# Weighted sum of expert outputs: a ring of token slots, interleaved VectorE sums, weights loaded once, 2 MiB stores, and three terms of the last eight tokens on TensorE

## The chip, the cores and the metric

The kernel runs on one core of a Trainium2 chip; the other cores are idle. The metric is the device time in microseconds (us) of one execution. Before the change three timed runs gave 721.29, 721.71 and 721.99 us; their median, 721.71 us, is the time to compare with.

## The reference

For 16 x 1024 = 16384 tokens there are eight expert rows of 512 float32 values and eight weights. The output row of a token is the weighted sum of its eight rows:

```python
def reference(expert_outputs, combine_weights):
    # expert_outputs (16, 1024, 8, 512) f32, combine_weights (16, 1024, 8) f32
    weights = combine_weights[..., np.newaxis]
    return np.sum(expert_outputs * weights, axis=2).astype(np.float32)
```

The core reads 268.4 MB of expert rows and 0.5 MB of weights, and writes 33.6 MB.

## The kernel before

A token of 16 KB (eight experts, 2 KB each) lies in one SBUF partition. The kernel cuts the tokens into 64 steps of 256: partition p of step n holds the two neighbouring tokens 256n + 2p and 256n + 2p + 1, so a load (line 56) is 4 MiB, 32 KB for each partition, and the whole of it is one contiguous piece of DRAM. The last two steps (`K_TAIL`) are loaded as two DMAs of 2 MiB, one for each j (line 59). Loads of even steps are issued by SyncE (SP), those of odd steps by ScalarE (ACT); each of the two has a DMA queue of its own. The 8 KB of weights of a step come by a small DMA from GpSimd (line 60). Four input buffers are used, and step n + 3 is loaded while step n is worked on.

For each token slot j of a step, VectorE makes the first product with a `tensor_scalar` (line 77) and adds the seven others with one `scalar_tensor_tensor` each (line 83): out = row times weight plus the sum so far, in one instruction over 128 partitions by 512 columns. Each sum is a chain of eight dependent instructions, and the second token's chain begins after the first's. The 512 KB of a step are then stored (line 92) by the queue that did not load this step, 4 KB for each partition.

The last two steps, 62 and 63, are different (lines 94 to 141). ScalarE multiplies experts 4 to 7 into bfloat16 (line 111), VectorE sums experts 0 to 3 in float32 (lines 116 and 122), adds the four products in bfloat16 (lines 130 and 135) and adds both halves (line 138). SP stores every half step by itself, 256 KB (line 141).

The order on each engine's instruction stream comes from the tile framework: it orders the instructions by a schedule of its own and sets the semaphores between them. A DMA is issued when the waits of its instruction have passed; what stands behind it on the same engine's stream waits with it. The waits follow the regions that instructions read and write, not whole tiles: at the end of the run ScalarE works on one half of a step while the other half is still under way.

Of the kernel before, what the change touches and what calls it, by code (L numbers as in the profile page):

```python
# [1 line left out]

# [4 lines left out]


@with_exitstack  # L10
def kernel(
    ctx: ExitStack,
    tc: tile.TileContext,
    expert_outputs: bass.AP,
    combine_weights: bass.AP,
    out: bass.AP,
):
    nc = tc.nc
    fp32 = mybir.dt.float32
    bf16 = mybir.dt.bfloat16  # L20

    B, S, E, D = expert_outputs.shape
    T = B * S
    P = 128
    J = 2
    n_steps = T // (P * J)

    eo_blk = expert_outputs.rearrange("b s e d -> (b s) e d").rearrange(
        "(n p j) e d -> n p j e d", p=P, j=J
    )  # L30
    w_blk = combine_weights.rearrange("b s e -> (b s) e").rearrange(
        "(n p j) e -> n p j e", p=P, j=J
    )
    o_blk = out.rearrange("b s d -> (b s) d").rearrange(
        "(n p j) d -> n p j d", p=P, j=J
    )

    in_pool = ctx.enter_context(tc.tile_pool(name="in_pool", bufs=4))
    w_pool = ctx.enter_context(tc.tile_pool(name="w_pool", bufs=4))
    out_pool = ctx.enter_context(tc.tile_pool(name="out_pool", bufs=4))  # L40
    prod_pool = ctx.enter_context(tc.tile_pool(name="prod_pool", bufs=2))

    ES = E // 2
    K_TAIL = 2

    load_engines = [nc.sync, nc.scalar]

    LA = 3
    in_tiles: list[bass.AP | None] = [None] * n_steps
    w_tiles: list[bass.AP | None] = [None] * n_steps  # L50

    def issue_load(m: int) -> None:
        in_t = in_pool.tile([P, J, E, D], fp32, name="in_t")
        w_t = w_pool.tile([P, J, E], fp32, name="w_t")
        if m < n_steps - K_TAIL:
            load_engines[m % 2].dma_start(out=in_t, in_=eo_blk[m])
        else:
            for j in range(J):
                load_engines[m % 2].dma_start(out=in_t[:, j], in_=eo_blk[m, :, j])
        nc.gpsimd.dma_start(out=w_t, in_=w_blk[m])  # L60
        in_tiles[m] = in_t
        w_tiles[m] = w_t

    for m in range(min(LA, n_steps)):
        issue_load(m)

    for n in range(n_steps):
        if n + LA < n_steps:
            issue_load(n + LA)
        if n >= n_steps - K_TAIL:  # L70
            continue
        in_tile = in_tiles[n]
        w_tile = w_tiles[n]
        acc = out_pool.tile([P, J, D], fp32)

        for j in range(J):
            nc.vector.tensor_scalar_mul(  # L77
                out=acc[:, j, :],
                in0=in_tile[:, j, 0, :],
                scalar1=w_tile[:, j, 0:1],  # L80
            )
            for e in range(1, E):
                nc.vector.scalar_tensor_tensor(  # L83
                    out=acc[:, j, :],
                    in0=in_tile[:, j, e, :],
                    scalar=w_tile[:, j, e : e + 1],
                    in1=acc[:, j, :],
                    op0=mybir.AluOpType.mult,
                    op1=mybir.AluOpType.add,
                )  # L90

        load_engines[(n + 1) % 2].dma_start(out=o_blk[n], in_=acc)  # L92

    tail_steps = list(range(n_steps - K_TAIL, n_steps))
    tail_accs = {}
    tail_prods = {}
    for n in tail_steps:
        acc = out_pool.tile([P, J, D], fp32, name="acc")
        prods = prod_pool.tile([P, J, E - ES, D], bf16, name="prods")
        tail_accs[n] = acc  # L100
        tail_prods[n] = prods

    for j in range(J):
        for n in tail_steps:
            in_tile = in_tiles[n]
            w_tile = w_tiles[n]
            acc = tail_accs[n]
            prods = tail_prods[n]

            for e in range(ES, E):  # L110
                nc.scalar.mul(  # L111
                    out=prods[:, j, e - ES, :],
                    in_=in_tile[:, j, e, :],
                    mul=w_tile[:, j, e : e + 1],
                )
            nc.vector.tensor_scalar_mul(  # L116
                out=acc[:, j, :],
                in0=in_tile[:, j, 0, :],
                scalar1=w_tile[:, j, 0:1],
            )  # L120
            for e in range(1, ES):
                nc.vector.scalar_tensor_tensor(  # L122
                    out=acc[:, j, :],
                    in0=in_tile[:, j, e, :],
                    scalar=w_tile[:, j, e : e + 1],
                    in1=acc[:, j, :],
                    op0=mybir.AluOpType.mult,
                    op1=mybir.AluOpType.add,
                )
            nc.vector.tensor_add(  # L130
                out=prods[:, j, 0:2, :],
                in0=prods[:, j, 0:2, :],
                in1=prods[:, j, 2:4, :],
            )
            nc.vector.tensor_add(  # L135
                out=prods[:, j, 0, :], in0=prods[:, j, 0, :], in1=prods[:, j, 1, :]
            )
            nc.vector.tensor_add(  # L138
                out=acc[:, j, :], in0=acc[:, j, :], in1=prods[:, j, 0, :]
            )  # L140
            nc.sync.dma_start(out=o_blk[n, :, j], in_=acc[:, j, :])


# [1 line left out]
_INS = ['expert_outputs', 'combine_weights']  # L145
_OUTS = [((16, 1024, 512), 'float32')]


# [23 lines left out]
```

## Time and profile before

| | |
|---|---|
| timed runs | 721.29, 721.71, 721.99 us |
| span of the profiled execution, first to last instruction | 720.4 us |
| VectorE busy | 644.4 us (89%) |
| ScalarE busy | 11.4 us (2%) |
| GpSimd busy | 35.8 us (5%), of which 35.6 us are the 64 weight loads of line 60 |
| TensorE | not used |
| DRAM traffic | 268.96 MB read, 33.55 MB written, 420 GB/s over the span |
| L83, 868 scalar_tensor_tensor | mean 743 ns |
| L77, 124 tensor_scalar | mean 482 ns |

The profile is of one execution; the page gives its span, and the three timed runs lie 0.9 to 1.6 us above that span. "Busy" is the time in which an engine executed instructions. A DMA's packets are worked off by 16 DMA engines; the DMA share is their mean busy share. Successive VectorE instructions overlap a little: fourteen of line 83 take 9.36 us in the timeline, 0.66 us from start to start, although each is shown as 743 ns long. Below, this distance from start to start is called a step.

### The profile page before, as it was taken

How to read it: one execution, taken by the hardware profiler on the slowest of the kernel's cores; microseconds unless marked ns; L12 is line 12 of the kernel's file. 1: busy time of each engine (PE TensorE's matmuls, PEld its weight loads, DVE VectorE, ACT ScalarE, POOL GpSimd, SP SyncE). 2: the span in 40 equal slices, each digit the busy share in tenths (PEclk: the TensorE clock that was granted, in tenths of full speed). 3: DMA queues.
4: the chain of work that ended last, by engine and by line, in shares of the span. 5: the costliest groups of instructions: out<-in, count | busy, mean ns of one | idle time of the engine just before them, and what ended most of it. 6: DMA issues, size and time to landing. Idle time of an engine off the chain costs nothing.

```text
span 720.4 us, 1532 instructions
## 1 busy us (share of the span) xinstructions
DVE 644.4 (89%) x1020; ACT 11.4 (2%) x17; POOL 35.8 (5%) x68
## 2 busy tenths in 40 slices
DVE  0799999999998999989998999989998999999977
ACT  0000000000000000000000000000000000000023
POOL 1000000000000000000000000000000000000000
DMA  9999999999999999999999999999999999999993
GB/s 380 437 416 451 427 426 430 427 424 439 443 431 426 426 423 431 438 436 434 431 423 426 435 430 442 432 424 427 430 429 432 442 431 428 430 425 428 433 359 120
DMA packets 21068, 302.63 MB, mean 420 GB/s; under 512 B 3136, under 2 KB 4160, under 8 KB 12608
## 3 DMA queue, kind: packets, MB, share of 16 engines
q1 hardware_dynamic: 9792, 151.52, 49.2%
q10 hardware_dynamic: 9216, 150.47, 48.9%
q0 software_dynamic: 2048, 0.53, 0.3%
q14 instruction: 12, 0.10, 0.0%
HBM read 268.96 MB, written 33.55 MB: 420 GB/s over the span
## 4 chain that ended last, share of the span: by engine, by line
DMA 63%; DVE 35%; issue 1%; DVEq 0%; SPq 0%
DMA out_dram<-acc 56%; DVE acc L83 30%; DMA in_t<-in_expert_outputs_dram 8%; DVE acc L77 3%; DVE acc L122 1%; DVE acc L138 0%; DVE prods L130 0%; DVE acc L116 0%; DVE prods L135 0%; DVEq L77 0%; DVEq L116 0%; SPq L92 0%
## 5 line engine op out<-in xcount | busy, mean ns | idle before, releaser
L83 DVE SCALAR_TENSOR_TENSOR acc<-in_t,w_t,acc 128x512 f32<-128x512 f32 x868 | 580.1, 743 | 0.0
L77 DVE TENSOR_SCALAR acc<-in_t,w_t 128x512 f32<-128x512 f32 x124 | 54.6, 482 | 66.3 <-DMA in_t<-in_expert_outputs_dram 43.4
L60 POOL DMA_DIRECT2D w_t<-in_combine_weights_dram x64 | 35.6, 556 | 637.7 <-DVE acc L83 636.9
L111 ACT ACT_TABLE_LOAD x1 | 1.3, 1283 | 690.6 <-DMA in_t<-in_expert_outputs_dram 690.6
L111 ACT ACTIVATE prods<-in_t,w_t 128x512 bf16<-128x512 f32 x16 | 10.1, 709 | 9.0 <-DMA in_t<-in_expert_outputs_dram 9.0
L122 DVE SCALAR_TENSOR_TENSOR acc<-in_t,w_t,acc 128x512 f32<-128x512 f32 x12 | 8.9, 745 | 0.0
L116 DVE TENSOR_SCALAR acc<-in_t,w_t 128x512 f32<-128x512 f32 x4 | 1.9, 481 | 5.3 <-DMA out_dram<-acc 5.3
L138 DVE TENSOR_TENSOR acc<-acc,prods 128x512 f32<-128x512 f32 x4 | 2.8, 688 | 0.0
L130 DVE TENSOR_TENSOR prods<-prods 128x1024 bf16<-128x1024 bf16 x4 | 2.7, 683 | 0.0
L135 DVE TENSOR_TENSOR prods<-prods 128x512 bf16<-128x512 bf16 x4 | 1.7, 417 | 0.0
L156 POOL MEMSET const-float32-0.0<- 128x1 f32 x1 | 0.1, 99 | 0.2 <-issue 0.2
L156 POOL MEMSET const-bfloat16-1.0<- 128x1 bf16 x1 | 0.1, 102 | 0.0
L156 POOL MEMSET const-float32-1.0<- 128x1 f32 x1 | 0.1, 99 | 0.0
L156 POOL MEMSET const-uint8-127<- 128x1 uint8 x1 | 0.1, 99 | 0.0
## 6 DMA issues: line engine op xcount, KB each, us to landing
in_t<-in_expert_outputs_dram ACTq DMA_DIRECT2D x31, 4096.0 KB, 33.5
in_t<-in_expert_outputs_dram SPq DMA_DIRECT2D x31, 4096.0 KB, 33.3
out_dram<-acc ACTq DMA_DIRECT2D x31, 512.0 KB, 33.5
out_dram<-acc SPq DMA_DIRECT2D x31, 512.0 KB, 33.4
in_t<-in_expert_outputs_dram SPq DMA_DIRECT2D x2, 2048.0 KB, 31.2
in_t<-in_expert_outputs_dram ACTq DMA_DIRECT2D x2, 2048.0 KB, 13.9
w_t<-in_combine_weights_dram POOLq DMA_DIRECT2D x64, 8.0 KB, 6.9
out_dram<-acc SPq DMA_DIRECT2D x4, 256.0 KB, 3.0
```

The costliest lines, as they stand in the source:

```text
L60: nc.gpsimd.dma_start(out=w_t, in_=w_blk[m])
L77: nc.vector.tensor_scalar_mul(out=acc[:, j, :], in0=in_tile[:, j, 0, :], scalar1=w_tile[:, j, 0:1],)
L83: nc.vector.scalar_tensor_tensor(out=acc[:, j, :], in0=in_tile[:, j, e, :], scalar=w_tile[:, j, e : e + 1], in1=acc[:, j, :], op0=mybir.Al ...
L111: nc.scalar.mul(out=prods[:, j, e - ES, :], in_=in_tile[:, j, e, :], mul=w_tile[:, j, e : e + 1],)
L116: nc.vector.tensor_scalar_mul(out=acc[:, j, :], in0=in_tile[:, j, 0, :], scalar1=w_tile[:, j, 0:1],)
L122: nc.vector.scalar_tensor_tensor(out=acc[:, j, :], in0=in_tile[:, j, e, :], scalar=w_tile[:, j, e : e + 1], in1=acc[:, j, :], op0=mybir.Al ...
L130: nc.vector.tensor_add(out=prods[:, j, 0:2, :], in0=prods[:, j, 0:2, :], in1=prods[:, j, 2:4, :],)
L135: nc.vector.tensor_add(out=prods[:, j, 0, :], in0=prods[:, j, 0, :], in1=prods[:, j, 1, :])
L138: nc.vector.tensor_add(out=acc[:, j, :], in0=acc[:, j, :], in1=prods[:, j, 0, :])
L156: nc = _bacc.Bacc("TRN2", target_bir_lowering=False, num_devices=1)
```

## The change

The kernel's middle is rewritten.

- **Layout.** Partition p now holds eight neighbouring tokens of each of 16 blocks (`G = 8`, 1024 tokens a block), 128 tokens in all, numbered i = 0 to 127 along the partition. A load is still two tokens for each partition, 4 MiB, 32 KB from each of 128 places in DRAM, but these places are now 128 KB apart.
- **Ring.** One tile `ring` has ten token slots; token i uses slot i % 10. Five loads can be in flight or in use, where it was four. All loads are issued by SP. Tokens 126 and 127 come in two and four pieces.
- **Weights.** All 0.5 MB are loaded by the first DMA of SP, in runs of 256 bytes.
- **First product.** ScalarE writes expert 0's product of each token into `acc`, one pair ahead of VectorE.
- **Two chains in turn.** VectorE adds experts 1 to 7 to the two tokens of a pair alternately.
- **Stores.** ScalarE issues one 2 MiB store for every eight tokens (16 KB for each partition), then one of 1 MiB for tokens 120 to 123; SP issues one of 512 KB for 124 and 125 and two of 256 KB for 126 and 127.
- **Last eight tokens.** For tokens 120 to 127 ScalarE makes three 128x128 float32 diagonal matrices from the weights, and TensorE sums experts 0 to 2 in PSUM with three float32 matmuls of 512 columns. VectorE adds experts 3 to 7, the first of them onto the sum in PSUM. The bfloat16 tail is gone.

`pin` keeps an instruction behind all that was written earlier for the same engine. The core of the diff, with the removed middle left out:

```diff
-    J = 2
-    n_steps = T // (P * J)
+    G = 8
+    N = T // (P * G)
+    T_P = N * G
+    SLOTS = 10
+    PE_TOKENS = 8
+    PE_EXPERTS = 3
...
+    x = expert_outputs.rearrange("b s e d -> (b s) e d").rearrange(
+        "(n p g) e d -> n p g e d", p=P, g=G
+    )
...
+    ring = one.tile([P, SLOTS, E, D], fp32, name="ring")
+    acc = one.tile([P, 2 * G, D], fp32, name="acc")
+    w_t = one.tile([P, T_P, E], fp32, name="w_t")
+    ident = one.tile([P, P], fp32, name="ident")
...
+    for t in range(BULK, T_P - 2, 2):
+        loads += [(t, 2, 0, E)]
+    loads += [(T_P - 2, 1, 0, 4), (T_P - 2, 1, 4, 8)]
+    loads += [(T_P - 1, 1, 0, 3), (T_P - 1, 1, 3, 5), (T_P - 1, 1, 5, 7), (T_P - 1, 1, 7, 8)]
...
+    def first(i):
+        s, a = i % SLOTS, i % (2 * G)
+        if i < T_P - PE_TOKENS:
+            pin(nc.scalar.mul(out=acc[:, a], in_=ring[:, s, 0], mul=w_t[:, i, 0:1]))
+            return
+        ps = ps_pool.tile([P, D], fp32, name="ps")
+        for e in range(PE_EXPERTS):
+            diag = diag_pool.tile([P, P], fp32, name="diag")
+            pin(nc.scalar.mul(out=diag, in_=ident, mul=w_t[:, i, e : e + 1]))
+            nc.tensor.matmul(
+                ps, lhsT=diag, rhs=ring[:, s, e], start=e == 0, stop=e == PE_EXPERTS - 1
+            )
+        sums[i] = ps
+
+    def term(i, e):
...
+            before, e0 = (sums[i] if e == PE_EXPERTS else acc[:, a]), PE_EXPERTS
+        if e >= e0:
+            pin(
+                nc.vector.scalar_tensor_tensor(
+                    out=acc[:, a],
+                    in0=ring[:, s, e],
+                    scalar=w_t[:, i, e : e + 1],
+                    in1=before,
...
+    pin(nc.sync.dma_start(out=w_t.rearrange("p (n g) e -> p n (g e)", g=G), in_=w))
+    make_identity(nc, ident)
+    load_until(SLOTS - 2)
+    for i in (0, 1):
+        first(i)
+    for i in range(0, T_P, 2):
+        load_until(i + SLOTS)
+        for k in (i + 2, i + 3):
+            if k < T_P:
+                first(k)
+        for e in range(E):
+            for k in (i, i + 1):
+                term(k, e)
+        end = i + 2
+        if end <= T_P - G and end % G == 0:
+            store(end - G, G, nc.scalar)
+        elif end == T_P - 4:
+            store(end - 4, 4, nc.scalar)
+        elif end == T_P - 2:
+            store(end - 2, 2, nc.sync)
+        elif end == T_P:
+            store(end - 2, 1, nc.sync)
+            store(end - 1, 1, nc.sync)
```

`load_until(t)` issues, in order, the loads of all tokens below t that are not yet issued; `store(i, m, queue)` stores m tokens from token i on.

## The prediction

> **What bounds the kernel now.** I read the page's slices and queues first, then the busy times by stage, then the waits of VectorE, and last the timeline of the end. From the page:
>
> ```profile
> DVE  0799999999998999989998999989998999999977
> ...
> DMA  9999999999999999999999999999999999999993
> ...
> q1 hardware_dynamic: 9792, 151.52, 49.2%
> q10 hardware_dynamic: 9216, 150.47, 48.9%
> q0 software_dynamic: 2048, 0.53, 0.3%
> ```
>
> VectorE looks full, but the 16 DMA engines are fuller: the three queues' packets fill 98.4% of the span. The table by stage has length, then busy us of VectorE, ScalarE and GpSimd, clock, DMA share, GB/s:
>
> ```profile
> 0.00:2.00 2.00, 0.00 (x0) 0.00 (x0) 0.96 (x6) 1.00 0.70 197
> 2.00:30.00 28.00, 7.06 (x12) 0.00 (x0) 1.50 (x3) 1.00 0.98 418
> ...
> 200.00:400.00 200.00, 183.10 (x289) 0.00 (x0) 9.65 (x18) 1.00 1.01 431
> ...
> 685.00:690.00 5.00, 5.00 (x9) 0.00 (x0) 0.00 (x0) 1.00 0.90 378
> 690.00:692.00 2.00, 2.00 (x4) 1.42 (x2) 0.00 (x0) 1.00 0.53 125
> 692.00:704.00 12.00, 6.66 (x13) 5.17 (x9) 0.00 (x0) 1.00 0.94 366
> 704.00:721.00 17.00, 12.01 (x21) 4.83 (x8) 0.00 (x0) 1.00 0.28 107
> ```
>
> From 30 to 685 us the share is 1.01 at 431 GB/s: DMA is the bound, and VectorE waits for it (183 of 200 us busy). VectorE's waits say so too:
>
> ```profile
> DVE acc L77 <- DMA in_t<-in_expert_outputs_dram: 43.4, 25, 22.9
> DVE acc L77 <- DMA out_dram<-acc: 22.9, 24, 1.9
> ```
>
> Past 685 us the DMA engines run dry while the computation ends. The timeline shows how:
>
> ```profile
> 690.72 0.82 ACTq L59 DMA_DIRECT2D in_t<-in_expert_outputs_dram  x2
> ...
> 708.41 2.56 ACT L111 ACTIVATE prods<-in_t,w_t 128x512 bf16<-128x512 f32 x4 [2.14 <-DMA in_t<-in_expert_outputs_dram]
> ...
> 715.36 0.69 DVE L138 TENSOR_TENSOR acc<-acc,prods 128x512 f32<-128x512 f32 x1
> ```
>
> The last two loads are issued at 690.72, when little else is under way; the last lands at 708.41; VectorE ends at 716.05; the span ends 4.35 us later (store and closing).
>
> So the span has three terms. By the packet records of the trace (duration by size), a packet of 32 KB takes 1213 ns, 16 KB 611, 8 KB 309, 4 KB 159, 2 KB 86, 512 B 27, and one of the 16 completion writes of a DMA 9: about 8.4 ns each plus 0.0368 ns a byte. All packets together are 709.4 us on each of 16 engines, which at the overlap of the middle (100.65 us of packets in 100 us) is 704.8 us. The first data packets start at 1.9 us. The rest, 720.4 - 704.8 - 1.9 = **13.7 us, is idle DMA**, all of it after 685 us.
>
> **The change, part by part.** *DMA work.* Stores: 32 MiB went as 4 KB and 2 KB packets, 81.7 us on each engine; after it, 15 x 128 packets of 16 KB x 611 ns / 16 = 73.3, 128 of 8 KB 2.5, 128 of 4 KB 1.3, 256 of 2 KB 1.4: 78.4. Loads: 623.8 in all, some of the last 16 KB packets being slow (mean 703 ns); after it, 63 x 128 x 1213 ns / 16 = 611.4, plus tokens 126 and 127 in 8, 6, 4 and 2 KB packets 10.1, plus 1.2 for slow first packets as now: 622.6. Weights: 1024 packets of 512 B, 1.7, against 2048 of 256 B, by the fit 17.8 ns each, 2.3. Completion writes: 3136 of 9 ns, 1.8, against 89 DMAs x 16, 0.8. With 0.4 for instructions: 704.5, in place of 709.4; divided by 1.0065, **700.0 us, 4.8 us less**.
>
> *One load queue.* All loads stand in SP's queue, behind no store. From 694 to 698 us q10 alone moved 430 GB/s, so one queue fills the engines; I cost it at nothing. If it did not, four loads in flight (39 us of data) could not help. The ring frees two slots when a pair is done, 10 us after its landing; those four loads hide that.
>
> *Loads 128 KB apart in place of 32 KB.* No row has this distance. Below: no gain, since the packets' 1213 ns have no spread (the 90th percentile is 1213 in nearly every stretch of 40 us). Above: the slow 16 KB packets at the end, 703 against 611 ns, 15%, which would be 90 us. I take nothing, since 1213 ns is the row of nearly all packets, and keep a rival. The Trainium skill speaks against this edit: "DMA: Bandwidth & Descriptors", section "Latency and other measured facts", lists DRAM copies at 512 KB between the partitions' rows at 207 GB/s, at 2 MiB at 164, where padded rows reach 214. By its 512 KB row, 3% slow, 611 us of loads would cost an estimated 18 us more; it gives no 128 KB row, and no trace here shows one.
>
> *VectorE.* Removed: 124 first products. Added: none; 7 steps a token remain, 14 x 0.66 = 9.24 us a pair, where now a step of 256 takes 10.16 (673.77 to 683.93). The DMA work of a pair is (9.70 + 1.22) / 1.0065 = 10.85 us, so VectorE stays hidden. Two chains in turn gain nothing: L122 to L122, dependent, is 0.66 us from start to start, and L122 to L130, independent, 0.66 as well. First products go to ScalarE, 0.64 a step (four in 2.56), 1.3 us a pair, ahead of VectorE. ScalarE's stores wait for VectorE's pair, and behind them stand the first products of the pair after next: hidden by VectorE's work on the pair between.
>
> *Start.* SP issues the weights first. A DMA of 128 pieces takes 0.34 us to issue; 2048 pieces take between that and 16 x 0.34 = 5.4 us, with DMA idle for what passes the 2.3 us of transfer. I take 0.5, nearer to the row, and 0.5 for a late engine at the end (at 667.07 the last of 16 completions of a load stood 0.6 us behind the others). GpSimd's 64 DMAs go; nothing waited for them late.
>
> *Tail.* Only the stores of 124 to 127 remain after the last load: 2.65 us of DMA work. So the last piece lands at **L** = 1.9 + (704.5 - 2.65) / 1.0065 + 1.0 = 700.2. Pair 124 lands before it by the pieces of 126 and 127 and the 1 MiB store, (10.1 + 2.5) / 1.0065 = 12.5 us: 687.7. From there TensorE has twelve matmuls (124 to 127) one after another. The weights' diagonals don't need the loads. No row shows a matmul. Below it lies the cheapest step on 512 columns, 0.33 us (L135); above, three ScalarE steps, one for taking in the 128x128 matrix and two for the columns, 1.92. I take two steps, **m = 1.28 us**, in the middle. The sum of 127 is then ready at 687.7 + 12m = 703.1. VectorE's order is 126, 127 by turns, so after it nine steps remain: 5.94 + 0.1 for the semaphore and 0.1 of the last one's length. End of VectorE 709.2, and 4.35 us as now: **span 713.6**, that is 698.2 + 12m. With m below 1.03 the first piece of 127 decides, which lands (4.95 + 1.87 + 2.5) / 1.0065 = 9.3 us after pair 124 and has three matmuls behind it: 707.5 + 3m, so 708.5 at m = 0.33. Idle DMA is then 11.7 us where it was 13.7, so most of the gain is DMA work, not the tail.
>
> Of the price of a matmul the Trainium skill has this: "FP8 and Floating Point Precision", section "TensorE Precision Notes", gives true float32 four passes. With "TensorE: Matmul & The Clock Gate", section "Back-to-back issue gap", N / 2.4 ns warm and N / 1.2 cold, that is an estimated 0.85 or 1.71 us, and a span of 710.1 or 718.7; bursts of six with pauses between, as here, may run cold. No run here shows either.
>
> **Against the timed runs.** The median lies 1.3 us above the profiled span (721.71 - 720.4). The forecast is 713.6 + 1.3 = **714.9 us**.
>
> **Rivals.**
> - *TensorE sets the end.* For: twelve matmuls stand in a row, and the tail before had none. It decides from m = 1.85 us (698.2 + 12m = 720.4); at 2.2 us the time is 698.2 + 26.4 + 1.3 = 725.9, slower. Against: L is 7 us earlier, and some matmuls can hide under VectorE's lag.
> - *Spread reads slow the packets.* Each DMA engine takes 504 big load packets; 13 ns more each, 1.1%, undoes 6.8 us. At 2%, 24 ns, the time is 714.9 + 12.2 = 727. Against: the packets show no sign of a DRAM limit.
> - *A store waits for a load's landing.* Now SP's store waits 14.1 us in all for other stores' landings, which no data asks for; DMAs seem to share a few completion counters in turn. If ScalarE's 2 MiB store at token 119 waits so for a late load, the diagonals behind it come late, TensorE starts perhaps 6 us late: 721, no change.
> - *TensorE nearly hidden* (m under 1.03): 707.5 + 3m + 1.3, from 709.8 to 711.9.
>
> **How the numbers follow.** This measurement can tell 0.2%, 1.4 us, from no change. Forecast (m 1.03 to 1.85): 0.52. TensorE nearly hidden: 0.22. Late store, no change: 0.04, with 0.01 of it faster. TensorE slow: 0.12, of which 0.01 within 0.2%. Slow packets: 0.10, of which 0.01 within 0.2%. Faster 0.52 + 0.22 + 0.01 = 0.75; same 0.03 + 0.01 + 0.01 = 0.05; slower 0.11 + 0.09 = 0.20. The range runs from 709 (nearly hidden) to 724, past m = 1.92 (722.5), and leaves out slow packets and most of slow TensorE, some 0.18.
>
> **What would show it.** Right: 431 GB/s from about 5 us to the last load, 32 KB packets at 1213 ns, the last load landing near 700, VectorE's waits on DMA larger than now, a matmul of 1.0 to 1.6 us. Wrong: large packets above 1226 ns; VectorE waiting for TensorE past 705; DMA share below 1.0 in the middle, which would mean that slots come free too late; a first load issued past 4 us.

## The result, and the profile after

The changed kernel takes 721.85 us (four runs, 721.26 to 722.18), the kernel before 721.59 us in the same session. The ratio is 1.0002, 95% interval 0.9988 to 1.0016: no difference. The forecast was 714.9 us with a range from 709 to 724; the time lies in the range, but the gain of about 1% did not come. The profiled execution has a span of 719.6 us, where the prediction worked out 713.6.

The page of the changed kernel, VectorE and DMA by slice and the queues (packets, MB, share of 16 engines):

```profile
DVE  0997896988979888897878969789697897988657
...
DMA  9999999999999999999999999999999999999991
...
q1 hardware_dynamic: 12432, 270.01, 87.5%
q10 hardware_dynamic: 2304, 32.51, 10.6%
q14 instruction: 9, 0.07, 0.0%
```

The page is not much different: DMA still fills the span, and VectorE has more holes (588.6 us busy in place of 644.4). The stages, with the same columns as before plus TensorE and its weight loads ahead of VectorE:

```profile
0.00:2.00 2.00, 0.00 (x0) 0.00 (x0) 0.00 (x0) 0.00 (x0) 0.70 (x6) 1.00 0.04 10
2.00:30.00 28.00, 0.00 (x0) 0.00 (x0) 11.65 (x18) 3.95 (x5) 0.00 (x0) 1.00 1.02 417
...
200.00:400.00 200.00, 0.00 (x0) 0.00 (x0) 170.73 (x256) 24.58 (x37) 0.00 (x0) 1.00 1.00 432
...
690.00:692.00 2.00, 1.32 (x4) 0.25 (x2) 0.65 (x1) 0.00 (x0) 0.00 (x0) 1.00 1.02 430
692.00:704.00 12.00, 8.02 (x13) 3.52 (x14) 6.22 (x11) 1.86 (x6) 0.00 (x0) 0.72 0.83 343
704.00:721.00 17.00, 5.04 (x12) 1.90 (x10) 12.59 (x19) 0.00 (x0) 0.00 (x0) 0.71 0.17 67
```

The middle runs at 432 GB/s, as forecast, with all loads in one queue. The hole at 690 us is gone (share 1.02 from 690 to 692 us, where it was 0.53). But the last 17 us are emptier than before (share 0.17, where it was 0.28). VectorE's waits, and then the timeline of the end:

```profile
DVE acc L111 <- ACT acc L92: 110.5, 57, 18.3
...
DVE acc L111 <- PE ps L98: 17.6, 6, 5.2
```

```profile
695.98 13.06 PE L98 MATMUL ps<-ring,diag 128*128 128x512 f32 x24 [4.66 <-DMA ring<-in_expert_outputs_dram]
...
701.36 0.75 DVE L111 SCALAR_TENSOR_TENSOR acc<-ring,w_t,ps 128x512 f32<-128x512 f32 x1 [3.95 <-PE ps L98]
...
703.93 0.75 DVE L111 SCALAR_TENSOR_TENSOR acc<-ring,w_t,ps 128x512 f32<-128x512 f32 x1 [1.83 <-PE ps L98]
...
704.60 5.38 DVE L111 SCALAR_TENSOR_TENSOR acc<-ring,w_t,acc 128x512 f32<-128x512 f32 x8
...
709.90 1.40 DVE L111 SCALAR_TENSOR_TENSOR acc<-ring,w_t,ps 128x512 f32<-128x512 f32 x2
...
711.21 5.38 DVE L111 SCALAR_TENSOR_TENSOR acc<-ring,w_t,acc 128x512 f32<-128x512 f32 x8
```

VectorE's 110.5 us of waiting for ScalarE are waits for loads at second hand: ScalarE, which makes the first products, itself waited 565.6 us for landings. TensorE starts on pair 124 when its load lands, at 695.98; the prediction had 687.7. That is 8.3 us, more than the whole miss of 6.0 us in the span. From there everything runs on without waiting for a load.

Why does pair 124 land so late, when the DMA engines moved as many bytes a second as forecast? The answer is in the completion records. A load is worked off by 16 DMA engines, and each reports when it is done with its part; the load has landed when the last has reported (the semaphore moves some 0.4 us after the report). These are the times of all 16 reports, in us, for one ordinary 4 MiB load of each kernel:

```
before   655.3 655.3 655.4 655.5 655.5 655.5 655.5 655.5 655.5 655.5 655.5 655.6 655.6 655.8 655.8          662.1
changed  654.6 654.9 654.9 654.9 654.9 655.0 655.0 655.0 655.1 655.4 655.5 656.3 656.6 656.6 657.3          661.4
```

In both kernels one DMA engine is 4 to 6 us behind the other fifteen. The lag grows through the run, by 0.6 to 1.0 us at a time. In the kernel before, the sixteenth report stands 0.1 us behind the middle one at 53 us, 0.8 at 64, 1.7 at 140, 2.5 at 217, 3.2 at 305, 4.1 at 382, 5.0 at 469, 5.8 at 546 and 6.5 at 634 us. Queue 14 (instruction fetches) has twelve records of 8 KB in this span. Eight of them stand at 56.8, 137.1, 213.4, 301.9, 379.3, 467.9, 545.5 and 633.9 us, one ahead of each rise of the lag, and the trace has 119 to 137 VectorE instructions between two of them, those that only wait included, 129 on average. At the other four (323.8, 345.8, 433.3 and 717.9 us) the lag does not rise; they have no such spacing, so they are probably fetches of other engines.

In the changed kernel one 32 KB packet beside each of the nine fetches takes 1593 to 1875 ns in place of 1213. There the last engine is 1.5 us late from the first loads on, and the lag rises by about 1 us at five of the nine fetches: after 246.6, 336.1, 435.4, 523.6 and 621.6 us, to 6.3 us. For the last load, the 2 KB packets of token 127, fourteen engines end by 700.9 us, one at 702.5, and one at **707.8**. For pair 124 the middle report stands at 689.0 us and the last at 695.4.

So the theory after the result is **lag**: VectorE's instruction fetches ride on one of the 16 DMA engines, each sets that engine back by about 1 us, and at the end all wait for it. The records do not name the engine of a packet, so this needs experiments. The rivals that were tried against it are **spread reads** (the distance of 128 KB slows packets) and **TensorE tail** (the cold matmuls set the end).

### The profile page after: what moved, and what is told of

It is laid out like the page before. It is cut to its first block, busy times and chain, and to the rows that moved or that the text cites. A ratio compares the mean times of both kernels' runs of the same rounds, so it can differ in the third digit from the quotient of the medians.

```text
span 719.6 us, 1429 instructions
## 1 busy us (share of the span) xinstructions
PE 28.0 (4%) x48; PEld 11.5 (2%) x48; DVE 588.6 (82%) x880; ACT 89.1 (12%) x145; POOL 0.7 (0%) x6
## 4 chain that ended last, share of the span: by engine, by line
DMA 91%; DVE 4%; another core or an unknown queue 1%; PE 1%; ACT 1%; issue 0%; SPq 0%; DVEq 0%; ACTq 0%
DMA ring<-in_expert_outputs_dram 91%; DVE acc L111 4%; PE ps L98 1%; ACT acc L92 1%; SPq L83 0%; DVEq L173 0%; SPq L125 0%; ACTq L92 0%; DVEq L111 0%
## 5 line engine op out<-in xcount | busy, mean ns | idle before, releaser
L111 DVE SCALAR_TENSOR_TENSOR acc<-ring,w_t,acc 128x512 f32<-128x512 f32 x872 | 583.1, 745 | 110.5 <-ACT acc L92 110.5
L92 ACT ACTIVATE acc<-ring,w_t 128x512 f32<-128x512 f32 x120 | 80.0, 714 | 565.6 <-DMA ring<-in_expert_outputs_dram 565.6
L98 PE MATMUL ps<-ring,diag 128*128 128x512 f32 x48 | 28.0, 749 | 681.0 <-DMA ring<-in_expert_outputs_dram 681.0
L98 PEld LDWEIGHTS ps<-ring,diag 128*128 128x128 f32 x48 | 11.5, 247 | 696.7 <-issue 695.2
L111 DVE SCALAR_TENSOR_TENSOR acc<-ring,w_t,ps 128x512 f32<-128x512 f32 x8 | 5.9, 744 | 17.6 <-PE ps L98 17.6
L97 ACT ACTIVATE diag<-ident,w_t 128x128 f32<-128x128 f32 x24 | 7.9, 390 | 28.7 <-DVE acc L111 25.0
```

What stands on the lines that cost most here:

```text
L92: pin(nc.scalar.mul(out=acc[:, a], in_=ring[:, s, 0], mul=w_t[:, i, 0:1]))
L97: pin(nc.scalar.mul(out=diag, in_=ident, mul=w_t[:, i, e : e + 1]))
L98: nc.tensor.matmul(ps, lhsT=diag, rhs=ring[:, s, e], start=e == 0, stop=e == PE_EXPERTS - 1)
L111: nc.vector.scalar_tensor_tensor(out=acc[:, a], in0=ring[:, s, e], scalar=w_t[:, i, e : e + 1], in1=before, op0=mult, op1=add,)
```

## The experiments

Each is an edit of the changed kernel. "To the kernel before" is the ratio of the times with its 95% interval.

**Which engine.** Six tiny loads are put into SP's queue, in the pass of the loop for pair 100.

```diff
+        if i == 100:
+            for r, (k, c) in enumerate(((1, 32), (2, 48), (4, 64), (8, 80), (15, 96), (16, 112))):
+                pin(nc.sync.dma_start(out=small[0:k, r, 0:c], in_=x[0, 0:k, 0, 0, 0:c]))
```

> The changed kernel with six tiny loads added in SP's queue before pair 100, over 1, 2, 4, 8, 15 and 16 partitions, so that they run on 1, 2, 4, 8, 15 and 16 DMA engines. In the changed kernel 15 completions of a late load come within about 3 us and the sixteenth some 5 to 6 us after the median. If the late one is always the same DMA engine, the tiny loads that include it have one packet that starts 4 to 6 us after their others, and those without it have none; so the place of the engine is bracketed. If the lateness wandered between engines, it would show in no tiny load or in any. The time itself should stay within 1 us of the changed kernel's 721.85 us.

One run took 722.04 us. The starts of the packets of each tiny load, in us (of 15 and 16 only the last are shown):

```
 1 partition   601.24
 2             601.25 603.61
 4             601.27 601.72 603.62 607.17
 8             601.29 601.50 601.53 601.74 602.53 602.54 603.64 607.20
15             ... 603.59 603.67 607.22
16             ... 603.62 603.69 607.24
```

The late packet is there from 4 partitions on and is always a single one, 3.5 us behind the next latest. So at this moment one DMA engine alone is late, and it is among those that a load of 4 partitions takes and a load of 2 does not. That it is the same engine from start to end is not shown by this run; the steady growth of the lag speaks for it.

**More instructions on VectorE, or on GpSimd.**

```diff
+        if i < 112:
+            for r in range(10):
+                pin(nc.vector.memset(tiny[:, r : r + 1], 0.0))
```

> The changed kernel with ten more VectorE instructions of one column in each of the first 56 pairs, 560 in all, 4.4 blocks of 128 instructions. VectorE has 1.4 us to spare in a pair, so its own work stays hidden. Theory lag (instruction fetches of VectorE ride on one of the 16 DMA engines, each costs this engine about 0.9 us, and the last load waits for it): four or five more fetches, the sixteenth completion some 4 us later than now, the time 3.5 to 4.5 us above the changed kernel's 721.85: about 726. Rival spread reads (the 128 KB distance slows packets): no change. Rival TensorE tail: no change.

726.91 us, 1.0079 (1.0065 to 1.0092) to the kernel before: 5.1 us more than the changed kernel. The page has five more fetches than the changed kernel's nine:

```profile
span 724.2 us, 1989 instructions
...
q14 instruction: 14, 0.11, 0.0%
```

The sixteenth report of a load at 655 us stands 10.9 us behind the middle, where it was 6.3; by then the next load's other reports are nearly all in. The last report of the last piece stands at 713.1 us, where it was 707.8. VectorE's own work grew by 10.3 us, hidden under 107 us of waits. That the longer work held back the loads themselves is ruled out: from 100 to 660 us both kernels move 432 GB/s, and the middle report of the load at 655 us stands within 0.2 us of the same time.

> The same 560 extra instructions, but on GpSimd, which is idle. Theory lag: also four or five more fetches, but if another engine's fetches ride on another DMA engine, which is not the last one, the time stays at 721.85 within 1 us; if they ride on the same one, it rises by 3 to 4 us as with VectorE. The rivals: no change.

With `nc.gpsimd.memset` in the same place: 721.83 us, 1.0012 (1.0003 to 1.0021), and no change to the changed kernel.

```profile
span 720.8 us, 1989 instructions
...
q14 instruction: 13, 0.11, 0.0%
```

Four more fetches, the same number of instructions in all, no more lag at the end (6.3 us at 655 us). What counts is not how many instructions are fetched but whose. GpSimd is not paced by loads and ran through its 560 in the first 24 us, and its fetches do cost something there: at 34 us the last report stands 3.7 us behind the middle, in the changed kernel 1.6. From 80 to 330 us it stays at 3.4 for an ordinary load, while VectorE's fetches go on; then it grows to the same 6.3. On one engine both would have added up, so GpSimd's fetches set back another engine, which by the end is not the last.

**Fewer instructions on VectorE.** Experts 4 to 7 of tokens 0 to 111 are left out of the sum.

```diff
-        if e >= e0:
+        if e >= e0 and (i >= 112 or e < 4):
```

> The changed kernel with less work on VectorE: tokens 0 to 111 get only experts 0 to 3, their last four terms are left out (448 instructions, 3.5 blocks of 128); loads, stores and the last 16 tokens are as they were. Theory lag: three or four fewer instruction fetches of VectorE, the slow DMA engine is some 3 us less behind at the end, and the time falls by 2.5 to 3.5 us, to about 719. If VectorE's instructions did not load a DMA engine, nothing changes, since VectorE waits for loads all the time: 721.85 within 0.7 us.

718.00 us, 0.9950 (0.9937 to 0.9963): 3.85 us less than the changed kernel, with the same loads and stores.

```profile
span 714.6 us, 981 instructions
...
q14 instruction: 6, 0.05, 0.0%
```

The lag at 655 us is 2.8 us. Dose and removal agree in the lag: 4.6 us more for 560 instructions and 3.5 us less for 448 are 8.2 and 7.8 ns an instruction, 1.0 us for each 128. The times, 5.06 and 3.85 us, would give 9.0 and 8.6 ns, but that agreement is partly luck, since the second holds something else:

```profile
693.53 10.54 PE L98 MATMUL ps<-ring,diag 128*128 128x512 f32 x24 [2.67 <-DMA ring<-in_expert_outputs_dram]
```

Pair 124 lands 2.4 us earlier than in the changed kernel (after one more fetch, at 662.8 us, the lag is 3.8 us), and the twelve matmuls, after a pause of 2.67 us in place of 4.66, take 2.5 us less. This profile is of the fastest of the four runs.

**Loads 32 KB apart.**

```diff
+    x2 = expert_outputs.rearrange("b s e d -> (b s) e d").rearrange(
+        "(n p g) e d -> n p g e d", p=P, g=2
+    )
...
-                dst, src = ring[:, s : s + m], x[n, :, g : g + m]
+                dst, src = ring[:, s : s + m], x2[i // 2]
...
-                dst, src = ring[:, s, e0:e1], x[n, :, g, e0:e1]
+                dst, src = ring[:, s, e0:e1], x2[i // 2, :, i % 2, e0:e1]
```

> The changed kernel with loads as they were before the change: each pair comes from one contiguous 4 MiB piece of DRAM, 32 KB apart for neighbouring partitions. Weights and stores keep the new layout, so tokens meet other tokens' weights and the output rows stand in other places. Rival spread reads: the big packets, of which half show 1214 to 1226 ns in the changed kernel, go back to 1213 all over; 504 packets on an engine times about 3 ns are 1.5 us, so the time falls by 1.5 us to 720.3, and by 8 us if the sixteenth completion's lag came from the distance. Theory lag: the late completion of 6 to 7 us stays, the time falls by at most 1.5 us.

721.96 us, 1.0008 (1.0000 to 1.0017). The mean of the 32 KB packets between 100 and 660 us is 1215.9 ns, in the changed kernel 1215.8; the lag at 655 us is 6.8 us. Distance between 32 and 128 KB is no cause: the rival falls, and with it the 1.5 us that were granted to it.

**Without TensorE.**

```diff
-    PE_TOKENS = 8
+    PE_TOKENS = 0
```

> The changed kernel without TensorE: the last eight tokens are summed like all others, expert 0 by ScalarE and seven terms by VectorE. Rival TensorE tail (six matmuls of pair 124 at a cold clock, 7.9 us before the second token's sum, are what the end waits for): after pair 124's landing 0.7 us of ScalarE and 28 VectorE steps of 0.66 us, 19.2 us, in place of 20.6 us now, so the time falls by 1 to 1.5 us, to about 720.6. Theory lag: the last pieces land at 706 to 708 us either way, VectorE then has 14 steps for 126 and 127 and ends about 715.3, where it now ends at 715.9: also 0.5 to 1.5 us faster. If TensorE did shorten the tail, as the change has it, the time rises by 4 us or more.

720.61 us, 0.9992 (0.9983 to 1.0001), 1.2 us less than the changed kernel, which the spread of its runs (719.58 to 722.38) does not tell clearly from no change. Both theories asked for a small gain, so it does not tell them apart. It does show that the diagonals bring nothing here: after pair 124 VectorE runs 28 steps in one piece.

```profile
696.68 18.64 DVE L111 SCALAR_TENSOR_TENSOR acc<-ring,w_t,acc 128x512 f32<-128x512 f32 x28 [2.16 <-ACT acc L92]
```

**Small stores.** Each pair up to token 119 is stored by itself, 512 KB in 4 KB packets.

```diff
-        if end <= T_P - G and end % G == 0:
-            store(end - G, G, nc.scalar)
+        if end <= T_P - G:
+            store(end - 2, 2, nc.scalar)
```

> The changed kernel with a 512 KB store for each pair up to token 119, 4 KB for each partition, in place of 2 MiB stores. The prediction had 16 KB packets save 3.3 us of DMA work on each engine: then 45 more DMAs and 4 KB packets cost 3.3 + 0.4 us, and the time rises to about 725.3. If the packets' sum does not set the end, because the load queue has room elsewhere, it stays at 721.85 within 0.7 us.

721.19 us, 1.0001 (0.9992 to 1.0010): the 3.7 us did not come. All packets together rise only from 705.6 to 707.4 us on each engine, in part because the 32 KB packets fall to a mean of 1213.6 ns (why is open). And the last loads have no 2 MiB store beside them: pair 124 lands at 695.76 us in spite of the longer sum. The profile is of the fastest of ten runs (718.75 to 723.16), and in this run TensorE helps too:

```profile
695.76 10.54 PE L98 MATMUL ps<-ring,diag 128*128 128x512 f32 x24 [2.43 <-DMA ring<-in_expert_outputs_dram]
```

After a pause of 2.43 us its twelve matmuls take 2.5 us less than the 13.06 of the changed kernel. How much of the median is owed to which, no run shows.

**Late stores.** The stores of tokens 112 to 119 and 120 to 123 are issued by SP and so stand behind all loads.

```diff
-            store(end - G, G, nc.scalar)
+            store(end - G, G, nc.sync if end == T_P - G else nc.scalar)
...
-            store(end - 4, 4, nc.scalar)
+            store(end - 4, 4, nc.sync)
```

> The changed kernel with the stores of tokens 112 to 119 and 120 to 123 (2 MiB and 1 MiB) issued by SP, so that they stand behind all loads in the same queue and not beside them in ScalarE's. Theory lag, with the chain from the last loads to the end: 3 MiB less beside the last loads, 7.4 us of DMA work; pair 124 lands 4.9 us earlier (691.1) and the last piece at about 700.5 on the slow engine; the late stores run in the 12 us in which the DMA engines are idle now. The time falls by 4 to 6 us, to about 717. If the sum of DMA work set the end, whatever its order, nothing changes: 721.85 within 0.7 us.

716.10 us, 0.9926 (0.9911 to 0.9941), faster than both kernels. The same bytes, in another order:

```profile
691.76 12.23 PE L98 MATMUL ps<-ring,diag 128*128 128x512 f32 x24 [4.34 <-DMA ring<-in_expert_outputs_dram]
...
706.17 5.38 DVE L111 SCALAR_TENSOR_TENSOR acc<-ring,w_t,acc 128x512 f32<-128x512 f32 x8
```

Pair 124 lands at 691.76 in place of 695.98, the last piece at 701.1 in place of 707.8, again with one engine alone behind. The sum of DMA work does not set the end; what stands beside and ahead of the last loads does. The lag is only part of this: the middle report of pair 124 comes 2.2 us earlier (686.8 for 689.0), its landing 4.2. What late stores would gain without a late engine was not tried.

**Three tries to shorten the tail behind the late stores.** First, the last four tokens summed one after the other:

> The kernel with the late stores, and for the last four tokens VectorE sums one token after the other, not two in turn. Pair 124 lands at 691.8 us in the run with late stores; TensorE's first sum is ready 4.55 us later at the slow clock. VectorE then has five steps for 124 while TensorE sums 125, and 20 steps of 0.66 us in all without a wait: it ends at 691.8 + 4.6 + 13.2 = 709.6 in place of 711.6. The time falls by 2 us from 716.1, to about 714. If the last landing (701.1) and not this chain set the end, nothing changes.

716.75 us, 0.9927 (0.9913 to 0.9942): no gain. The timeline shows why: four steps of one chain end 3.11 us after the first begins.

```profile
705.35 3.11 DVE L111 SCALAR_TENSOR_TENSOR acc<-ring,w_t,acc 128x512 f32<-128x512 f32 x4
...
708.38 0.74 DVE L111 SCALAR_TENSOR_TENSOR acc<-ring,w_t,ps 128x512 f32<-128x512 f32 x1
...
709.16 3.12 DVE L111 SCALAR_TENSOR_TENSOR acc<-ring,w_t,acc 128x512 f32<-128x512 f32 x4
```

A step that needs the one just before it takes 0.787 us ((3.11 - 0.75) / 3), a step of two chains in turn 0.66. Sixteen such steps cost 2 us, as much as the order saved.

Second, the same with twenty dummy matmuls ahead of pair 124:

```diff
+        if i == T_P - 4:
+            for r in range(20):
+                pin(nc.tensor.matmul(warm, lhsT=ident, rhs=ident, start=True, stop=True))
```

> As late_seq, and TensorE is kept busy between pairs 122 and 124 by twenty matmuls of the unit matrix with itself, whose result nobody reads. If a TensorE that just worked has the fast clock (three matmuls in 2.6 us, where they take 4.6 to 5.4 us after a pause), the first sum of pair 124 is ready 2.6 us after its landing and the time falls by 2 us more, to about 712. If the clock is slow whatever runs before, the dummies delay pair 124 or do nothing: 714 or more.

716.64 us, 0.9921 (0.9908 to 0.9934): the dummies ran until 693.9 us and kept pair 124 waiting, which had landed at 692.0. Third, ten dummies and two chains in turn:

> The kernel with the late stores, two chains in turn as in the change, and ten dummy matmuls of the unit matrix between pairs 122 and 124 (half of the twenty that held TensorE until 2.2 us after pair 124's landing). The first sum of pair 124 is ready 2.6 us after its landing, the second 5.2; then 9 and 10 VectorE steps of 0.66 us without a gap: VectorE ends at 691.6 + 5.2 + 12.6 = 709.4, in place of 711.6 with late stores alone. The time falls by 2 us from 716.1, to about 714. If VectorE's order or the landing of the last piece (701) holds it, it stays at 716.

715.99 us, 0.9924 (0.9910 to 0.9937). The clock did as expected, the first sum came 2.85 us after the landing in place of 4.55, but in the profiled execution pair 124 itself landed 1.5 us later (693.2). Whether the dummies' own instruction fetches did that was not tried.

**Late stores without TensorE.**

> The kernel with the late stores, without TensorE: all tokens are summed by ScalarE and VectorE. From pair 124's landing 0.75 us of ScalarE and 28 VectorE steps in 18.6 us, as the run without TensorE showed: VectorE ends at 691.8 + 19.4 = 711.2, where it ends at 711.6 with TensorE. The time is 715.7, within 1 us of the 716.1 with TensorE, so the diagonals bring nothing in this order.

716.00 us, 0.9921 (0.9908 to 0.9934). As expected, and the simplest of the five: no diagonals, no PSUM. The five versions with late stores can't be told apart (716.0 to 716.75).

## Why the prediction was wrong, point by point

- **The step that failed** stands under *Start*: "0.5 for a late engine at the end (at 667.07 the last of 16 completions of a load stood 0.6 us behind the others)". The reports had been read in groups of 16 by time. But the sixteenth report of a load comes so late that it stands among the next load's: the 662.1 that looked like an early report was the late one of the load before. The term is 7 us, not 0.5: fourteen engines end the loads by 700.9, near the forecast's L of 700.2, and the last at 707.8. The dose and the removal show whose lag it is. For pair 124, whose landing the end hangs on, it is 6.4 of the 8.3 us; its middle report, 689.0, is 1.3 us later than the forecast landing. DMA work, 1.1 us above forecast, may be most of that; it was not tested.
- **What went with it:** the 13.7 us of idle DMA before were taken for a fault of the old tail, which the change would cut to 11.7. Part of them is fifteen engines waiting for one (the lag is 6 to 7 us in both kernels at 655 us), and that stayed.
- **DMA work** fell from 709.4 to 705.6 us on each engine (forecast 704.5). The step was right as a sum and wrong as a price: small stores put work back and cost nothing, late stores took none away and gained 5.7 us. What counts is what the engines, and the late one above all, must do before the last load.
- **One load queue, spread reads, start:** right. 432 GB/s; no effect of 128 KB; the first big packets start at 3.7 us, where 4.2 less some overlap had been granted (1.9 + 2.3 for the weights; the first data packet of the kernel before starts at 1.7 us, not 1.9). The row-pitch rule of the Trainium skill ("DMA: Bandwidth & Descriptors", "Latency and other measured facts") speaks of 512 KB and more; at 128 KB these runs show nothing of it.
- **VectorE:** hidden, as said. But the evidence for "two chains in turn gain nothing" was wrong. The two L122 that stand together at 703.21 us belong to two tokens: one is the third of a token that has had two (695.73, 696.73), the other the first behind the L116 of 702.80. In the middle, too, the timeline shows two of L77 and then fourteen of L83 in steps of 0.66 us: the tokens of a step were taken in turn, not one chain after the other. A dependent step is 0.787, as the late stores with one chain at a time show.
- **TensorE:** m was mis-sized, in the safe direction: twelve matmuls took 13.06 us, 1.09 each, not 1.28. The first three took 5.50, 4.31 and 5.38 us after the pauses before pairs 120, 122 and 124, where the granted clock was about 0.7 (692 to 704 us), and 2.57 when TensorE had just worked: 1.4 to 1.8 and 0.86 each. The slowest and the fastest agree with the two figures worked out from the Trainium skill ("TensorE: Matmul & The Clock Gate", "Back-to-back issue gap", with "FP8 and Floating Point Precision", "TensorE Precision Notes"), 1.71 and 0.85. The formula 698.2 + 12m took the wrong chain, though: not 127's sum but VectorE's backlog from pair 124 on comes last. Measured: 695.98, six matmuls 7.95, then 19 steps 12.66, closing 3.0: 719.6. Forecast: 687.7, twelve matmuls 15.4, 9 steps 6.1, closing 4.35: 713.6. The three differences after the landing come to -2.2 us, the landing to +8.3.
- **Rivals:** the late store did not happen (ScalarE's 2 MiB store was issued at 672.06, right when VectorE was done with token 119), and TensorE was not slow. No rival named one DMA engine that all wait for by several us.

What stays open: which rule gives VectorE's fetches to that engine, whether a fetch costs as much beside other transfers than these loads, and why the 32 KB packets take 1214 to 1226 ns half of the time beside 2 MiB stores and 1213 beside small ones.

## What to carry to other kernels

When DMA bounds a kernel, ask when the slowest of the 16 engines is done, not their mean: group the completion reports by load, not by time. Here every 128 VectorE instructions cost one DMA engine about 1.0 us, so an instruction that is hidden on its own engine still cost time at the end. Stores that are not needed early went best behind the last load in the same queue, where the idle end hides them; that was worth 5.7 us here, where fewer and bigger packets were worth nothing that the runs could tell. And a profile is of one run: where the runs spread over 2 us or more, ask which of them it shows before you take its end for the median's.

## What the runs showed of the hardware

- VectorE's instruction fetches delay one DMA engine, 7.8 to 8.2 ns for each instruction (lag of a load at 655 us: 10.9, 6.3 and 2.8 us with 560 more, none and 448 fewer); 560 instructions on GpSimd left another engine 3.4 us behind and delayed no load that counted.
- A `scalar_tensor_tensor` of 128x512 float32 starts 0.66 us after an independent one and 0.787 us after one whose output it needs.
- A float32 matmul of 128x128 by 128x512 is two records in the trace; three such matmuls take 4.2 to 5.5 us after a pause of 3.7 to 5.8 us and 2.6 us while TensorE stays busy. After a pause of 2.1 to 2.7 us they stayed near 2.6 us in three runs and took 4.1 in one; with ten dummies that ended 2.1 us before, 2.85 us.
